# One decoder block on one core: row tile 2's modulation sums move from TensorE to VectorE, and the opening is put in a new order

## The chip, the cores and the metric

The kernel runs on one core of a Trainium2 chip. The metric is the device time of one execution in microseconds (us). Engines are named as the profile names them: PE (TensorE matmuls), PEld (its weight loads), DVE (VectorE), ACT (ScalarE), POOL (GpSimd) and SP (SyncE, which here only issues DMAs, in order).

## The reference, cut to what matters

The block computes six modulation vectors from `c`, normalises and modulates `x`, and multiplies the result by a wide matrix `w_in`; the rest (a state-space branch, attention, a gated merge, an MLP) follows and is not touched by the change.

```python
c_act = jax.nn.silu(c)
mod = c_act @ w_ada[l] + b_ada[l]                     # (1, 6 * 2048)
sh1, sc1, g1, sh2, sc2, g2 = jnp.split(mod, 6)
h = rms_norm(x, norm_mix_g[l]) * (1.0 + sc1) + sh1    # 256 x 2048
proj = h @ w_in[l]                                    # 2048 x (1024 + 3 * 1024 + 2 * 2048)
u, q, k, v, ga, gb = jnp.split(proj, split_at, axis=-1)
```

So no row of `h` exists before its entries of `sc1` and `sh1` do, and each of those entries is a sum over 2048 products of `w_ada` with `silu(c)`. Everything is in float32.

## The kernel before, in words

**Row tiles.** The 2048 model features are cut into 16 row tiles of 128, numbered 0 to 15. Row tile kt of `h` (128 features by 256 tokens, transposed) is made by `make_h1`: ScalarE applies scale `A1[kt]` and shift `B1[kt]` to the normalised `x`, then `split` stores it as a high part (ScalarE's cast, in `ah`) and a low part (VectorE's subtraction, in `al`).

**w_in tiles.** `w_in` is streamed in tiles of 128 x 1024 (512 KB each). A tile is loaded into `wraw` (seven buffers), split into `whi` (ScalarE cast) and `wlo` (VectorE subtraction, four buffers each), and multiplied in three passes: high by high, high by low, low by high. A q, k or u tile is 24 matmuls of 256 columns (`steps_t`, tile name pt, lines 270 to 272); a v or gate tile is 12 of 512 columns (`steps_n`, pn, lines 327 to 331). I count w_in tiles in the order in which the code streams them (`self.tno`): tiles 1 to 4 are q, k, v, u with row tile 0; then `duo` interleaves gate (`gp`) with row tiles 0 to 3 and u with row tiles 1 to 3 (tiles 5 to 11); then v, q with rows 1 to 3, and so on. The last rows, 14 and 15, are first used by tiles 51 and 52.

**Where the sums are made.** For row tiles 0 to 2 the sums run on TensorE: `ada_first` loads two 512 KB pieces of a host-side layout `wan` for the scale and two for the shift, multiplies them in 32-column strips (`adap`, 16 matmuls per vector, each counted twice in the trace since a float32 product runs as two passes), copies the 128 x 128 result to SBUF (`acopy`, ScalarE) and folds it with a ones column (`adac`). For row tile 3 and all later ones they run on VectorE: `ada_wide` loads two 512 KB pieces per row of 128 x 2048 from `wat`, and one instruction multiplies by `cb` (the broadcast `silu(c)`) and accumulates.

**What orders the work.** A planner orders the instructions of each engine by priority and simulated readiness. `high_priority` raises a block (by 300 for the w_in stream, by 3000 for the rows 0 to 3); `after(ins)` puts an instruction behind `ins` on `ins`'s own engine only. `self.gates` holds pairs (VectorE instruction, ScalarE instruction) that the next w_in tiles' splits must follow. `self.last` chains loads on SP. Lanes are lists of jobs, called in `step` after each w_in tile's matmuls: lane "second" (rate 1.0) makes row tiles 1 to 3, lane "ada" (rate 0.75) makes rows 4 to 15, with three empty jobs in front, and `want(kt)` pulls jobs early if row kt has not been written down yet when its first w_in tile is streamed.

In the kernel before, lane "second" fetches row 1 at tiles 3 and 4, sums it on TensorE behind tile 4, makes row 1 and then loads, sums and makes row 2 at tile 5 (sums behind tile 5's last matmul), and sums row 3 on VectorE in the steps after tiles 7 and 8. `ssm_params2` (two sines on ScalarE and some thirty small VectorE instructions) stands at tile 3.

Of the kernel before, what the change touches and what calls it, by code (L numbers as in the profile page):

```python
# [19 lines left out]
P = 128  # L20
# [57 lines left out]
class Kern:  # L78
# [111 lines left out]
    def stream(self, src, kts, c0, homes=()):  # L190
        homes = list(homes)
        kts, nxt = list(kts), None
        for i, kt in enumerate(kts):
            with self.tc.high_priority(offset=OFF):
                w = nxt if nxt is not None else self.load(src, kt, c0)
                nxt = None
                if self.raw:
                    self.raw(w)
                home = homes.pop(0) if homes else None
                if home:  # L200
                    hi, lo = home
                else:
                    hi = self.wp.tile([P, 1024], F32R, name="whi", tag="whi", bufs=4)
                    lo = self.wp.tile([P, 1024], F32R, name="wlo", tag="wlo", bufs=4)
                self.gate, self.hgate = self.gates.pop(0) if self.gates else (None, None)
                self.tno += 1
                if self.pend and self.pend[0][0] <= self.tno - 2:
                    self.gate = self.pend.pop(0)[1]
                self.split(hi, lo, w)
                self.wcast = self.done[-1][1]  # L210
                self.gate = self.hgate = None
                if self.look and i + 1 < len(kts):
                    self.look, nxt = False, self.load(src, kts[i + 1], c0)
# [41 lines left out]
    def steps_t(self, src, kts, c0, xh, xl, koff=0, mid={}, homes=(), seed=None):  # L255
        nc = self.nc
        banks = self.four("pt")
        full = self.seeded(banks, seed)
        n = len(kts)
        for i, (kt, hi, lo) in enumerate(self.flow(src, kts, c0, homes)):  # L260
            kx = kt - koff
            if i in mid:
                mid[i]()
            turn = self.mm if self.strict else None
            for blk in range(8):
                o = banks[blk // 2][:, (blk % 2) * S:(blk % 2 + 1) * S]
                c = slice(blk * P, (blk + 1) * P)
                st, sp = i == 0 and blk % 2 == 0 and not full, i == n - 1
                with self.after(turn):
                    nc.tensor.matmul(o, hi[:, c], xh[:, kx, :], start=st, stop=False, skip_group_check=True)  # L270
                    nc.tensor.matmul(o, hi[:, c], xl[:, kx, :], start=False, stop=False, skip_group_check=True)  # L271
                    self.mm = nc.tensor.matmul(o, lo[:, c], xh[:, kx, :], start=False, stop=sp,  # L272
                                               skip_group_check=True)
                if blk == 3:
                    self.mid = self.mm
            self.whi = hi
            yield banks
# [60 lines left out]
    def ada_first(self, j, kt, done, home=None, gate=None):  # L338
# [14 lines left out]
        def total(i):  # L353
            w = st.pop(i).rearrange("p (k n) -> p k n", k=8)
            if i == 0:
                st["p"] = self.aux("adap")
            p = st["p"][:, 0:P]
            with self.after(self.ss_last if self.early else gate):
                for k in range(8):
                    q = 32 * (k % 4)  # L360
                    m = nc.tensor.matmul(p[q:q + 32, :], self.cz[:, 8 * i + k, :], w[:, k, :], start=i == 0 and k < 4,
                                     stop=i == 1 and k > 3, tile_position=(0, q), skip_group_check=True)
            if i == 1:
                acc = self.s4[:, 512 + P * n:640 + P * n]
                self.acopy = nc.scalar.copy(acc, p)
                st["acc"], st["last"] = acc, m

        def fold(gate=None):
            pc = self.aux("adac")
            with self.after(gate):  # L370
                self.adac = nc.tensor.matmul(pc[:, 0:1], st["acc"], self.ones[:, 0:1], start=True, stop=True)
            done(pc[:, 0:1])
        return ([(lambda i=i: load(i), lambda i=i: total(i)) for i in range(2)], fold, lambda: st["last"])

    def ada_job(self, vec, k0, n, done, ring=None):
# [41 lines left out]
    def ada_wide(self, vec, k0, n, done, ring):  # L417
# [12 lines left out]
        def total(i):  # L430
            w = st.pop(i)
            with self.after(self.lead or self.done[-1][0]), self.after(self.floor):
                sm = v.scalar_tensor_tensor(w, w, 1.0, self.cb, op0=OP.mult, op1=OP.mult, accum_out=pc[:, i:i + 1])
            if k0 >= 8:
                self.pend.append((self.tno, sm))
            if i == n - 1:
                done(pc)
# [183 lines left out]
    def ssm_params(self):  # L621
# [30 lines left out]
        v.scalar_tensor_tensor(em1, ss, -1.0, em1, op0=OP.add, op1=OP.add)  # L652
        self.scan_in = (r, mag, em1, are, aim, tmp)

    def ssm_params2(self):
# [3 lines left out]
        with self.after(self.done[-1][1]):  # L659
            nc.scalar.activation(sh, r, AF.Sin, scale=0.5)  # L660
            nc.scalar.activation(sn, r, AF.Sin)
# [348 lines left out]
    def body(self):  # L1010
# [110 lines left out]
        homes = {1: regs[0:4], 2: regs[4:8]}  # L1121

        sums, h2 = {}, []

# [15 lines left out]
                                tot()  # L1140
            return f

        def third(i):
            def f():
                with self.tc.high_priority(offset=OF1):
                    if i == 0:
                        ring3 = [h.rearrange("p k c -> p (k c)") for h in h4]
                        sums[3] = (self.ada_wide(1, 3, 1, fin_scale(1, A1, lambda: self.gmix, 3, 1), ring3)
                                   + self.ada_wide(0, 3, 1, fin_shift(0, B1, 3, 1), ring3))
                    if i < 2:  # L1150
                        sums[3][i][0]()
                        self.last = self.wide_ld
                    if i:
                        self.lead = h2[0][0] if i == 1 else self.done[-2][0]
                        sums[3][i - 1][1]()
                        self.lead = None
                    if i == 2:
                        self.make_h1(3, A1, B1, 1)
                        self.floor = self.done[-1][0]
                        self.gates = [(self.shifted, None), (self.floor, None)]  # L1160
            return f

        def finish(kt):
            def f():
                with self.tc.high_priority(offset=OF1):
                    for units, fold, last in sums[kt]:
                        fold(sums[kt][1][2]())
                    self.make_h1(kt, A1, B1, 1)
                    self.force = self.adac
                    if kt == 1:  # L1170
                        self.gates += [(self.shifted, self.acopy)]
                    else:
                        h2.append(self.done[-1])
                        self.gates += [(self.shifted, None), h2[0]]
                        self.seedgate = h2[0][1]
            return f

        def params2():
            with self.after(self.done[-1][0]):
                self.ssm_params2()  # L1180

        def both(*fs):
            return lambda: [f() for f in fs]
# [22 lines left out]
        def evac(which, banks, add):  # L1206
# [4 lines left out]
            for b in range(4):  # L1211
# [1 line left out]
                if which == 4 and add:  # L1213
                    d = self.ga[:, b // 2, (b % 2) * 512:(b % 2) * 512 + 512]
                with self.after(self.wcast):
                    nc.scalar.copy(d, view(banks[b]))  # L1216

        g1t = {}

# [51 lines left out]
        self.want = want  # L1271
        nop = lambda: None
        units = []
        wide = [h[:, 2 * i:2 * i + 2, :].rearrange("p k c -> p (k c)") for h in (hv, hq) for i in range(2)]
        ring = wide * 6
        for k0 in range(4, KT, 2):
            units += mod1(k0, 2, ring) + [(None, hjob(k0))]
# [3 lines left out]
        def drain(n):  # L1281
            while len(ready) < n:
                self.lanes["ada"][0].pop(0)()

        self.drain = drain
        self.lane("second", [nop, nop, both(fetch(1, 0), params2), both(fetch(1, 1), follow(1)),
                              both(finish(1), fetch(2, 0), fetch(2, 1), follow(2), finish(2)), third(0), third(1),
                              third(2)], 1.0)
        self.lane("xr", [lambda: self.scale1(1, self.done[-1][0], 3)]
                  + [lambda k0=k0: self.scale1(k0, self.done[-1][0]) for k0 in range(4, KT, 2)], 2.0)  # L1290
        jobs = self.ringed(units, free)
        self.lane("ada", [nop] * 3 + jobs + late, R1)
# [32 lines left out]
        self.cover = True  # L1325
        self.look = True
        qkvu(order[3], order[4])
        duo(order[4], order[5], (0, 0, 0, 1, 1, 0, 1), order[6], lambda: h2[0][1], 4)
        self.cover = False
        qkvu(order[6], order[7])  # L1330
        qkvu(order[7], order[8], True)
# [409 lines left out]
```

## Time and profile before

| | |
|---|---|
| median of 3 runs | 1356.92 us (1356.69 to 1357.32) |
| profiled execution, its own time | 1356.04 us |
| its span, first to last instruction | 1354.3 us |
| PE, DVE, ACT busy | 99%, 77%, 55% of the span |
| mean granted TensorE clock | 0.999 |

The span is what the trace's clock runs over; 1.74 us of the execution's own time lie outside it. Busy time on PE is modelled for pipelined matmuls, so I read PE by the starts of successive matmuls instead: work that issues back to back has equal distances between starts.

### The profile page before, as it was taken

How to read it: one execution, taken by the hardware profiler on the slowest of the kernel's cores; microseconds unless marked ns; L12 is line 12 of the kernel's file. 1: busy time of each engine (PE TensorE's matmuls, PEld its weight loads, DVE VectorE, ACT ScalarE, POOL GpSimd, SP SyncE). 2: the span in 40 equal slices, each digit the busy share in tenths (PEclk: the TensorE clock that was granted, in tenths of full speed). 3: DMA queues.
4: the chain of work that ended last, by engine and by line, in shares of the span. 5: the costliest groups of instructions: out<-in, count | busy, mean ns of one | idle time of the engine just before them, and what ended most of it. 6: DMA issues, size and time to landing. Idle time of an engine off the chain costs nothing.

```text
span 1354.3 us, 21608 instructions
## 1 busy us (share of the span) xinstructions
PE 1342.8 (99%) x8276; PEld 1167.6 (86%) x8276; DVE 1038.2 (77%) x1441; ACT 751.1 (55%) x1045; POOL 49.0 (4%) x105
## 2 busy tenths in 40 slices
PE   9999999999999999999999999999999999999997
PEld 8898899788888988888998888888888888888886
DVE  7888998677987888988888967686765555565687
ACT  7768656766558543455546656353554544535544
POOL 0000004200004000000000000000000000000000
PEclk9999999999999999999999999999999999999999
DMA  9999977975568888997899897888878666566552
GB/s 377 407 408 409 389 252 210 306 241 180 159 215 262 314 283 300 334 337 290 291 342 339 296 235 263 220 281 258 276 243 230 190 187 197 187 188 198 176 196 83
DMA packets 116856, 357.09 MB, mean 264 GB/s; under 512 B 16728, under 2 KB 16864, under 8 KB 116464
## 3 DMA queue, kind: packets, MB, share of 16 engines
q1 hardware_dynamic: 113056, 348.83, 76.5%
q0 software_dynamic: 3120, 5.70, 1.4%
q8 instruction: 65, 1.06, 0.3%
q10 hardware_dynamic: 576, 1.18, 0.3%
q14 instruction: 39, 0.32, 0.1%
HBM read 350.79 MB, written 2.51 MB: 261 GB/s over the span
## 4 chain that ended last, share of the span: by engine, by line
PE 95%; ACT 2%; DMA 2%; DVE 1%; issue 0%; SPq 0%; ACTq 0%; DVEq 0%
PE pn L327 18%; PE pn L329 18%; PE pn L331 18%; PE pd L289 14%; PE pd L293 7%; PE pt L270 6%; PE pt L272 6%; PE pt L271 6%; DMA wraw<-in_w_in_dram 1%; PE ys L992 1%; ACT whi L184 1%; DMA xt<-in_xt_dram 0%; PE trh L834 0%; PE vr L954 0%; PE rk L794 0%
## 5 line engine op out<-in xcount | busy, mean ns | idle before, releaser
L186 DVE TENSOR_TENSOR wlo<-wraw,whi 128x1024 fp32r<-128x1024 f32 x448 | 546.2, 1224 | 254.4 <-ACT whi L184 253.0
L184 ACT CAST whi<-wraw 128x1024 fp32r<-128x1024 f32 (+1 forms) x449 | 467.3, 1051 | 479.6 <-PE pn L329 214.3
L289 PE MATMUL pd<-h2h,whi 128*128 128x512 f32 x800 | 207.3, 393 | 0.2 <-ACT whi L184 0.2
L327 PE MATMUL pn<-whi,ff 128*128 128x512 f32 x496 | 193.3, 390 | 0.0
L329 PE MATMUL pn<-whi,ff 128*128 128x512 f32 x496 | 193.3, 390 | 0.0
L331 PE MATMUL pn<-wlo,ff 128*128 128x512 f32 x496 | 190.9, 390 | 0.0
L289 PEld LDWEIGHTS pd<-h2h,whi 128*128 128x128 f32 x800 | 141.3, 189 | 22.9 <-ACT whi L184 0.4
L391 DVE SCALAR_TENSOR_TENSOR wraw<-wraw,cb 128x1024 f32<-128x1024 f32 x128 | 156.2, 1221 | 0.0
L327 PE MATMUL pn<-whi,ah 128*128 128x512 f32 x320 | 126.7, 400 | 0.8 <-ACT qk L1216 0.4
L329 PE MATMUL pn<-whi,ah 128*128 128x512 f32 x320 | 125.5, 392 | 0.0
L293 PEld LDWEIGHTS pd<-h2h,wlo 128*128 128x128 f32 x800 | 114.8, 190 | 11.5
L293 PE MATMUL pd<-h2h,wlo 128*128 128x256 f32 x800 | 117.9, 282 | 0.0
L331 PE MATMUL pn<-wlo,ah 128*128 128x512 f32 x320 | 115.9, 392 | 0.4 <-DVE wlo L186 0.4
L331 PEld LDWEIGHTS pn<-wlo,ff 128*128 128x128 f32 x496 | 93.1, 188 | 19.5
L329 PEld LDWEIGHTS pn<-whi,ff 128*128 128x128 f32 x496 | 93.2, 188 | 19.0
L327 PEld LDWEIGHTS pn<-whi,ff 128*128 128x128 f32 x496 | 93.1, 188 | 19.1
L270 PE MATMUL pt<-ah,whi 128*128 128x256 f32 x384 | 105.9, 286 | 0.2 <-DVE tz L611 0.2
L271 PE MATMUL pt<-ah,whi 128*128 128x256 f32 x384 | 104.9, 283 | 0.0
L272 PE MATMUL pt<-ah,wlo 128*128 128x256 f32 x384 | 95.9, 284 | 0.8 <-DVE wlo L186 0.7
L270 PEld LDWEIGHTS pt<-ah,whi 128*128 128x128 f32 x384 | 73.4, 192 | 1.8 <-ACT whi L184 0.7
L271 PEld LDWEIGHTS pt<-ah,whi 128*128 128x128 f32 x384 | 73.4, 192 | 0.2
L327 PEld LDWEIGHTS pn<-whi,ah 128*128 128x128 f32 x320 | 59.9, 188 | 15.3 <-ACT whi L184 1.3
(386 smaller groups left out, 2009.3 us busy)
## 6 DMA issues: line engine op xcount, KB each, us to landing
wraw<-in_w_ff_dram SPq DMA_DIRECT2D x256, 512.0 KB, 4.8
wraw<-in_w_in_dram SPq DMA_DIRECT2D x128, 512.0 KB, 6.1
wraw<-in_wat_dram SPq DMA_DIRECT2D x128, 512.0 KB, 5.9
ahm<-in_wat_dram SPq DMA_DIRECT2D x48, 512.0 KB, 10.2
wraw<-in_w_out_dram SPq DMA_DIRECT2D x32, 512.0 KB, 6.5
wraw<-in_w_proj_attn_dram SPq DMA_DIRECT2D x16, 512.0 KB, 5.7
wraw<-in_w_proj_ssm_dram SPq DMA_DIRECT2D x16, 512.0 KB, 6.4
ahm<-in_wan_dram SPq DMA_DIRECT2D x8, 512.0 KB, 10.6
```

The lines of the kernel that those rows point to most:

```text
L184: h = self.nc.scalar.copy(hi[:, c], src[:, c])
L186: s = self.nc.vector.tensor_sub(lo, src, hi.bitcast(F32))
L270: nc.tensor.matmul(o, hi[:, c], xh[:, kx, :], start=st, stop=False, skip_group_check=True)
L271: nc.tensor.matmul(o, hi[:, c], xl[:, kx, :], start=False, stop=False, skip_group_check=True)
L272: self.mm = nc.tensor.matmul(o, lo[:, c], xh[:, kx, :], start=False, stop=sp, skip_group_check=True)
L289: nc.tensor.matmul(banks[blk], hi[:, cut(blk, k)], x2[:, ks[k], :, :], start=i + k == 0, stop=False, skip_group_check=True)
L293: self.mm = nc.tensor.matmul(banks[blk][:, S:2 * S], lo[:, cut(blk, k)], x2[:, ks[k], 0, :], start=False, stop=last and k == 1, skip_group ...
L327: nc.tensor.matmul(o, xh[:, kx, tk], hi[:, c], start=q == 0 and not full, stop=False, skip_group_check=full)
L329: nc.tensor.matmul(o, xl[:, kx, tk], hi[:, c], start=False, stop=False, skip_group_check=full)
L331: self.mm = last = nc.tensor.matmul(o, xh[:, kx, tk], lo[:, c], start=False, stop=q == n - 1, skip_group_check=full)
L391: v.scalar_tensor_tensor(w, w, 1.0, self.cb[:, (i % 2) * 1024:(i % 2 + 1) * 1024], op0=OP.mult, op1=OP.mult, accum_out=pc[:, i:i + 1])
L992: nc.tensor.matmul(p[q, c], self.cc[q, i, j].rearrange("p s c -> p (s c)"), self.sri[q, b % 2, i, c], start=i == 0, stop=False)
```

## The change

- Row tile 2's sums move from `ada_first` (TensorE) to `ada_wide` (VectorE, two instructions over 128 x 2048), with loads from `wat` instead of `wan` (four of 512 KB either way).
- Row 1 is fetched whole at tile 3, and its TensorE sums stand behind tile 3 instead of tile 4. Its copies to SBUF (`bring`) come only at the fold, behind the last evacuation copy (`self.moved`), and its fold stands behind the middle matmul of tile 4 (`self.mid`).
- The VectorE sums of row 2 are put between the splits of tiles 3 and 4 and of tiles 4 and 5; those of row 3 between the splits of tiles 7 and 8, and behind tile 8's. `behind` makes a w_in tile's split wait for the sum in front of it.
- `duo` takes u's row 1 before the gate's row 2. A unit's stored partial results are copied back (`seeded`) after its first w_in tile has been split, not before.
- `ssm_params2`'s sines stay at tile 3; its VectorE part moves to the step in front of tile 10.
- Lane "ada" has six empty jobs in front instead of three.

```diff
@@ stream
-                self.wcast = self.done[-1][1]
+                self.newest, self.wcast = self.done[-1]
@@ steps_t
-        full = self.seeded(banks, seed)
+        full, n = seed is not None, len(kts)
         for i, (kt, hi, lo) in enumerate(self.flow(src, kts, c0, homes)):
+            if i == 0:
+                self.seeded(banks, seed)
@@ ada_first
             if i == 1:
-                acc = self.s4[:, 512 + P * n:640 + P * n]
-                self.acopy = nc.scalar.copy(acc, p)
-                st["acc"], st["last"] = acc, m
+                st["last"] = m
+                if self.early:
+                    bring()
+        def bring(gate=None):
+            acc = st["acc"] = self.s4[:, 512 + P * n:640 + P * n]
+            with self.after(gate):
+                self.acopy = nc.scalar.copy(acc, st["p"][:, 0:P])
-        def fold(gate=None):
+        def fold(gate=None, then=None):
+            if "acc" not in st:
+                bring(self.moved)
...
-            done(pc[:, 0:1])
+            with self.after(then):
+                done(pc[:, 0:1])
@@ ada_wide
+            self.summed = sm
@@ body
+        def bring(kt, j):
+                    if j == 0:
+                        single(kt, wide[2:] if kt == 2 else [h.rearrange("p k c -> p (k c)") for h in h4])
+                    sums[kt][j][0]()
+                    self.last = self.wide_ld
+        def add(kt, j):
+                    self.lead = self.newest
+                    sums[kt][j][1]()
+                    self.lead = None
+        def behind(*gates):
+                self.gates += [g and (self.summed, None) or (None, None) for g in gates]
+        def modulate(kt):
+                    self.make_h1(kt, A1, B1, 1)
+                    h2.append(self.done[-1])
+        def last():
+            modulate(3)()
+            self.floor = self.done[-1][0]
+            self.gates += [(self.floor, None)]
+        def finish():
+                for units, fold, end in sums[1]:
+                    fold(self.mid, self.summed)
+                self.make_h1(1, A1, B1, 1)
+                h2.append(self.done[-1])
+                self.force = self.adac
+                self.seedgate = h2[0][1]
+        def first():
+            self.gates += [h2[0]]
@@ evac
-                    nc.scalar.copy(d, view(banks[b]))
+                    self.moved = nc.scalar.copy(d, view(banks[b]))
@@ lanes
-        self.lane("second", [nop, nop, both(fetch(1, 0), params2), both(fetch(1, 1), follow(1)),
-                              both(finish(1), fetch(2, 0), fetch(2, 1), follow(2), finish(2)), third(0), third(1),
-                              third(2)], 1.0)
+        self.lane("second", [nop, nop, both(fetch(1, 0), fetch(1, 1), follow(1), bring(2, 0), add(2, 0), behind(1),
+                                            angles),
+                             both(bring(2, 1), add(2, 1), behind(1), finish, first), behind(0),
+                             both(bring(3, 0), bring(3, 1), add(3, 0), behind(1), modulate(2)),
+                             both(add(3, 1), behind(0)), both(last, params2)], 1.0)
-        self.lane("ada", [nop] * 3 + jobs + late, R1)
+        self.lane("ada", [nop] * 6 + jobs + late, R1)
-        duo(order[4], order[5], (0, 0, 0, 1, 1, 0, 1), order[6], lambda: h2[0][1], 4)
+        duo(order[4], order[5], (0, 0, 1, 0, 1, 0, 1), order[6], lambda: h2[0][1], 4)
```

More of the change, by code (lines that the diff above doesn't have):

```diff
@@ L257, in steps_t @@
         banks = self.four("pt")
-        full = self.seeded(banks, seed)
-        n = len(kts)
+        full, n = seed is not None, len(kts)
         for i, (kt, hi, lo) in enumerate(self.flow(src, kts, c0, homes)):
             kx = kt - koff
+            if i == 0:
+                self.seeded(banks, seed)
             if i in mid:
@@ L653, in ssm_params, with ssm_angles @@
         self.scan_in = (r, mag, em1, are, aim, tmp)
+    def ssm_angles(self):
+        r, tmp = self.scan_in[0], self.scan_in[-1]
+        with self.after(self.wcast):
+            self.nc.scalar.activation(tmp(10), r, AF.Sin, scale=0.5)
+            self.nc.scalar.activation(tmp(11), r, AF.Sin)
     def ssm_params2(self):
@@ L658, in ssm_params2 @@
         sh, sn = tmp(10), tmp(11)
-        with self.after(self.done[-1][1]):
-            nc.scalar.activation(sh, r, AF.Sin, scale=0.5)
-            nc.scalar.activation(sn, r, AF.Sin)
         v.tensor_mul(sh, sh, sh)
@@ L1120, in body @@
         regs = [h[:, i, :] for h in (hv, hq) for i in range(4)]
-        homes = {1: regs[0:4], 2: regs[4:8]}
+        homes = {1: regs[0:4]}
+        wide = [h[:, 2 * i:2 * i + 2, :].rearrange("p k c -> p (k c)") for h in (hv, hq) for i in range(2)]
         sums, h2 = {}, []
@@ L1141, in follow, with single @@
             return f
-        def third(i):
+        def single(kt, ring):
+            sums[kt] = (self.ada_wide(1, kt, 1, fin_scale(1, A1, lambda: self.gmix, kt, 1), ring)
+                        + self.ada_wide(0, kt, 1, fin_shift(0, B1, kt, 1), ring))
+        def bring(kt, j):
             def f():
                 with self.tc.high_priority(offset=OF1):
[L1146 to L1160, printed above, removed]
@@ L1161, in third @@
+                    if j == 0:
+                        single(kt, wide[2:] if kt == 2 else [h.rearrange("p k c -> p (k c)") for h in h4])
+                    sums[kt][j][0]()
+                    self.last = self.wide_ld
             return f
-        def finish(kt):
+        def add(kt, j):
             def f():
                 with self.tc.high_priority(offset=OF1):
-                    for units, fold, last in sums[kt]:
-                        fold(sums[kt][1][2]())
-                    self.make_h1(kt, A1, B1, 1)
[L1169 to L1175, printed above, removed]
-            return f
+                    self.lead = self.newest
+                    sums[kt][j][1]()
+                    self.lead = None
+            return f
@@ new lines, in behind, with f @@
+        def behind(*gates):
+            def f():
+                self.gates += [g and (self.summed, None) or (None, None) for g in gates]
+            return f
+        def modulate(kt):
+            def f():
+                with self.tc.high_priority(offset=OF1):
+                    self.make_h1(kt, A1, B1, 1)
+                    h2.append(self.done[-1])
+            return f
+        def last():
+            modulate(3)()
+            self.floor = self.done[-1][0]
+            self.gates += [(self.floor, None)]
@@ L1178, in params2 @@
+        def finish():
+            with self.tc.high_priority(offset=OF1):
+                for units, fold, end in sums[1]:
[6 more added lines that the diff above has]
+            self.gates += [h2[0]]
         def params2():
-            with self.after(self.done[-1][0]):
+            with self.after(self.newest):
@@ L1180, in params2, with angles @@
                 self.ssm_params2()
+        def angles():
+            with self.after(self.newest):
+                self.ssm_angles()
         def both(*fs):
@@ L1273, in body @@
         units = []
-        wide = [h[:, 2 * i:2 * i + 2, :].rearrange("p k c -> p (k c)") for h in (hv, hq) for i in range(2)]
         ring = wide * 6
```

## The prediction

> **What bounds the kernel now.** I read the page first, then the busy times of a few stretches, then the order of PE's matmuls and of SP's loads in the opening. The page's first line and its chain of work:
>
> ```profile
> span 1354.3 us, 21608 instructions
> ```
>
> ```profile
> PE 95%; ACT 2%; DMA 2%; DVE 1%; issue 0%; SPq 0%; ACTq 0%; DVEq 0%
> ```
>
> The chain that ends last is matmuls, so an edit pays if it takes work or waits out of PE's queue, and only as long as PE doesn't then wait for something else. What that could be shows in the stretches (each engine's busy us, then PE clock, DMA share, GB/s):
>
> ```profile
> 27.60:57.40 29.80, 29.40 (x285) 25.48 (x284) 22.95 (x47) 21.44 (x39) 0.52 (x1) 1.00 1.03 406
> ...
> 66.00:165.00 99.00, 98.96 (x684) 92.01 (x683) 89.81 (x98) 67.44 (x102) 1.04 (x2) 1.00 1.03 408
> 165.00:1354.30 1189.30, 1180.53 (x7072) 1020.71 (x7070) 895.10 (x1197) 634.20 (x863) 45.32 (x89) 1.00 0.75 245
> ```
>
> The reader is to see three things. All that is edited runs between 27.6 and 57.4, where VectorE is idle for 29.80 - 22.95 = 6.85 us. To 165 us the DMA moves 406 to 408 GB/s without a pause, and from 66 to 165 VectorE has only 9 us in 99 to spare. Behind 165 the DMA falls to 245 GB/s and PE alone sets the time, so a lead that PE still has at 165 lasts to the end. The granted clock is 1.00 throughout.
>
> **PE's part.** The groups of PE's instructions from 27.6 to 57.4 that aren't products with w_in (count, busy us, mean ns), and its instructions in order of time:
>
> ```profile
> L361 PE MATMUL adap<-ahm,tz 128*32 128x128 f32 x128 | 3.9, 274 | 0.0
> L371 PE MATMUL adac<-s 128*128 128x1 f32 x8 | 1.1, 208 | 0.0
> L115 PE MATMUL pt<-ah 128*128 128x512 f32 x3 | 1.1, 419 | 0.0
> ```
>
> ```profile
> 27.59 0.28 PE L270 MATMUL pt<-ah,whi 128*128 128x256 f32 x1
> ...
> 36.09 1.95 PE L361 MATMUL adap<-ahm,tz 128*32 128x128 f32 x64
> 37.97 0.96 PE L327 MATMUL pn<-whi,ah 128*128 128x512 f32 x3
> 38.77 0.28 PE L371 MATMUL adac<-s 128*128 128x1 f32 x2
> 38.91 0.48 PE L329 MATMUL pn<-whi,ah 128*128 128x512 f32 x1
> ...
> 49.76 0.39 PE L272 MATMUL pt<-ah,wlo 128*128 128x256 f32 x1 [0.29 <-DVE wlo L186]
> ...
> 51.77 1.09 PE L327 MATMUL pn<-whi,ah 128*128 128x512 f32 x4
> ...
> 54.52 0.28 PE L270 MATMUL pt<-ah,whi 128*128 128x256 f32 x1
> ...
> 57.39 0.40 PE L327 MATMUL pn<-whi,ah 128*128 128x512 f32 x1
> ```
>
> The 128 adap passes are rows 1 and 2; row 2's 64 hold PE from 36.09 to 37.97, 1.88 us. Its two folds cost 38.91 - 38.77 = 0.14 each, 0.28. Each of these three breaks also restarts the full-width matmuls; the first after such a break takes about 0.1 us more than its neighbours by the spacing of starts, which I put at 0.3 together. **Removed from PE: 1.9 + 0.3 + 0.3 = about 2.4 us.** Row 1's 64 passes only move from behind u's tile 4 to behind v's tile 3.
>
> From the same rows, a v or gate tile takes 54.52 - 51.77 = 2.75 us and a q, k or u tile 57.39 - 54.52 = 2.87 us.
>
> **SP's part.** The moved loads decide when tiles 4 and 5 land. SP's loads in order (start, time of the issues, name, count), and the time from issue to landing of row 3's loads, with the sum on VectorE that reads them:
>
> ```profile
> 8.99 1.61 SPq L349 DMA_DIRECT2D ahm<-in_wan_dram  x2
> 13.22 0.33 SPq L176 DMA_DIRECT2D wraw<-in_w_in_dram  x1
> 13.60 0.91 SPq L349 DMA_DIRECT2D ahm<-in_wan_dram  x2
> 15.44 3.31 SPq L176 DMA_DIRECT2D wraw<-in_w_in_dram  x2
> 19.55 4.11 SPq L349 DMA_DIRECT2D ahm<-in_wan_dram  x4
> ...
> 32.33 2.89 SPq L176 DMA_DIRECT2D wraw<-in_w_in_dram  x3
> 36.17 0.33 SPq L427 DMA_DIRECT2D ahm<-in_wat_dram  x1
> ```
>
> ```profile
> L433 DVE SCALAR_TENSOR_TENSOR ahs<-ahs,cb x2: 2285/2286/2286, 42.4 to 46.2; 128x2048 f32<-128x2048 f32 x2
> ...
> DMA to landing us min/median/max: 10.2/10.2/10.2
> ```
>
> Four issues take 4.11 us, the last 0.33 of it by itself: one 512 KB load each 1.26 us, the pace of the full DMA. Counted from 8.99, before has row 1 twice, tile 4, row 1 twice, tiles 5 and 6, and row 2 as loads 8 to 11 from 19.55. After, the fetch of row 1 and row 2's scale stand at priority 3000 in one step ahead of tile 4: row 1 as 1 to 4, row 2's scale as 5 and 6, tile 4 as 7, row 2's shift as 8 and 9, tiles 5, 6, 7 as 10 to 12, then row 3. With load 8 at 19.55, 10.2 to land and 1.26 between loads, row 2's scale is there at 27.2, tile 4 at 28.5, row 2's shift at 31.0, tile 5 at 32.3, tile 6 at 33.5. The bytes are the same, so the DMA gains or loses nothing; tile 4 is five microseconds later than before.
>
> ```profile
> 25.00 1.05 ACT L184 CAST whi<-wraw 128x1024 fp32r<-128x1024 f32 x1
> ```
>
> That is tile 4's cast now; 1.05 us is its price. After, tile 4 is cast by 29.55 and tile 5 by 33.35.
>
> **VectorE's part.** It gains two sums of 2.29 us, 4.6 us, in a stretch with 6.85 us idle. Both have landed when their place comes: row 2's scale is summed from 27.2 to 29.5, tile 4's split follows to 30.7; the shift is summed from 31.0 to 33.3, row 1's few scalars and tile 5's split follow to about 35. `ssm_params2`'s small operations move from the front of this stretch to its end, cost nothing while the idle time lasts, and would delay tile 10's split if it didn't. ScalarE loses two copies and has 29.80 - 21.44 = 8.4 us idle; the later `seeded` copies find their split done. POOL's bias load waits for a buffer that `ssm_params2` now holds longer, and nobody needs it in the opening.
>
> **The sum.** PE ends tile 3 at 27.59 as before; row 1's sums (landed long before) take it to 29.6, just when tile 4 has been cast; tile 4 to 32.4. Then it waits for tile 5's cast until 33.4, about 0.95 us: the one new wait. From there four gate tiles and three u tiles, 4 x 2.75 + 3 x 2.87 = 19.6, and the three L115 matmuls, about 0.8, without a wait: 53.8, with row 1's folds 53.9. Before that point stood at 57.39, so 3.5 us are gained: 2.4 of work, and the waits like that at 49.76, which vanish because their sums come earlier, less the new one. I take 0.3 off for first low-part matmuls that catch their split too soon: **3.2 us**.
>
> The new waits have no row of their own, so I bound them. If PE runs each tile's blocks strictly high, high, low, tile 4's first low matmul stands at 29.9 and waits to 30.7, and tile 5's stands at 33.9 and waits to 35.1: 2.0 us more, a gain of 1.2. If tile 5 has no wait at all (SP puts it ahead of row 2's shift), 4.4. I take the value near the upper end, since the row at 51.77 shows four high matmuls ahead of the first low one: PE's order already puts high parts first where a split is late.
>
> **Does the lead last to 165?** The tightest places of the DMA and of the last rows, in ScalarE's, VectorE's and PE's order:
>
> ```profile
> 160.30 1.05 ACT L184 CAST whi<-wraw 128x1024 fp32r<-128x1024 f32 x1 [2.79 <-DMA wraw<-in_w_in_dram]
> ```
>
> ```profile
> 165.04 0.69 DVE L186 TENSOR_TENSOR ah<-htmp,ah 128x512 fp32r<-128x512 f32 x1
> ```
>
> ```profile
> 166.12 0.39 PE L327 MATMUL pn<-whi,ah 128*128 128x512 f32 x1
> ...
> 171.56 0.39 PE L327 MATMUL pn<-whi,ah 128*128 128x512 f32 x1
> ```
>
> Tile 49's cast waits for its DMA, ends at 161.35 and is used at 166.12: a margin of 4.8 us. Rows 14 and 15 are done at 165.73 and used at 171.56 (tile 51): 5.8 us. A lead of 3.2 fits into both. The three extra empty jobs cost nothing at the front: row 4's first load stands at 36.17, directly behind tiles 9 to 11 (32.33, three loads), where the new place puts it too. At the back the list is pulled by `want`; writing both lists out, the last sum comes one tile later (behind tile 49's split instead of 48's) and rows 14 and 15 two, of which two times 2.8 less the lead still fits.
>
> In the profiled execution: span 1354.3 - 3.2 = 1351.1, its own time 1356.04 - 3.2 = 1352.8. The median of the runs lies 0.9 above that execution, so 1356.92 - 3.2 = **1353.7 us**. A change of 0.2%, 2.7 us, is about what a measurement of this kernel tells from none.
>
> **The rivals.** *Waits take the place (within 0.2%).* Tiles 4 and 5 wait for forced sums as in the lower bound: 1.2 us gained, 1355.7. For it speaks the wait at 49.76, where a split behind a sum did hold PE; against it, that PE had its high parts in front there and lost 0.29 only. The Trainium skill ("TensorE: Matmul & The Clock Gate", section "Architectural detail: the array is 16× 32×32, not 1× 128×128") says that VectorE's queue is strictly first in, first out; by that rule everything queued behind a sum whose row is late waits too, and no row here shows a sum that waited for its row.
>
> *The DMA is the bound (no change).* It is full to 165 us, so PE's lead is given back as w_in tiles stop landing in time: 1356.9. For it: 406 to 408 GB/s throughout and the 2.79 us wait of tile 49's cast. Against it: that cast is still 4.8 us ahead of PE, and the loads in front of it are the same. The Trainium skill ("Perfetto Trace Analysis", section "Identifying the Most-Contended Engine") has the engine with the highest occupancy, for DMA its share of the bandwidth, set the time; with the 435 GB/s that "DMA: Bandwidth & Descriptors", section "Where 436 GB/s comes from", gives as the ceiling, 408 is 94%, and the sum by that rule would be zero. I weigh it below the 4.8 us that the rows show in hand.
>
> *The later rows come too late (slower).* If the three empty jobs really shift every later sum by four tiles (three at 0.75 a tile), 4 x 2.87 = 11.5 us, rows 14 and 15 are ready at 165.73 + 11.5 = 177.2 against 171.56, and PE stands 5.7 us at tile 51: 1362.6. It decides from 5.8 us of delay on; half of the shift is a draw. For it: VectorE's 9 us spare in 99, and sums bound to the newest split. Against it: `want` and the one-tile count above.
>
> **How the numbers follow.** The forecast (2.2 to 4.4 gained, 1352.5 to 1354.7) has 0.62, of which 0.50 lies beyond 2.7 us; waits 0.13; DMA 0.12; late rows 0.13. So faster 0.50, within 0.2% 0.12 + 0.13 + 0.12 = 0.37, slower 0.13. The range: at the low end tile 49's whole margin is used, 1356.9 - 4.8 - 0.3 (the spread of the runs) = 1351.8; at the high end rows come 7.3 us late, 1.5 beyond the draw, 1358.4.
>
> **What would show it.** Right: row 2's adap and adac gone from PE, its two sums on VectorE before 34; tile 4's cast near 28.5; PE 3 us or more ahead at tile 12 (57.39 before) and still at tile 51 (171.56). Wrong: waits of PE over 0.5 us on `wlo` at tiles 4 to 8; a lead that shrinks between 66 and 165 with casts released by DMA; PE waiting for `ah` at tile 25 or 51.

## The result: slower by 0.6%, and the profile after

| | before | after |
|---|---|---|
| time, median of the runs (us) | 1357.06 (1355.58 to 1357.51) | 1365.27 (1364.35 to 1366.52) |
| span of the profiled execution (us) | 1354.3 | 1363.8 |

The ratio is 1.0062, with a 95% interval of 1.0049 to 1.0075: 8.2 us slower in the runs, 9.5 in the two profiled spans. Forecast were 3.2 us faster.

The opening itself went as forecast. The end of tile 11 and the next two tiles, in PE's order of time after the change:

```profile
54.03 0.28 PE L273 MATMUL pt<-ah,wlo 128*128 128x256 f32 x1
55.15 0.50 PE L328 MATMUL pn<-whi,ah 128*128 128x512 f32 x1 [0.84 <-ACT pn L237]
...
59.63 0.50 PE L328 MATMUL pn<-whi,ah 128*128 128x512 f32 x1 [1.40 <-ACT whi L184]
```

Tile 11's last matmul starts at 54.03, where 53.9 was forecast for the end of the tile. Its matmuls start 0.12 us apart, so tile 12 could start at 54.15; before, it started at 57.39. PE has a lead of about 3.2 us (0.35 of it already stood at tile 3, at 22.45 against 22.80). The bracket of the next line is the first bad sign: PE waits where it did not wait before. All waits of PE from 27 to 110 us (total, number, longest):

```profile
PE pt L272 <- DVE ah L186: 3.4, 1, 3.4
PE pt L271 <- ACT ah L184: 2.7, 1, 2.7
PE pn L328 <- ACT whi L184: 1.7, 2, 1.4
PE pn L328 <- ACT pn L237: 0.8, 1, 0.8
```

One `whi` wait, 0.3 us, is at tile 6 (36.81). The rest is in two places, read by the spacing of the matmuls: 2.6 us at tiles 12 and 13, and 6.3 us (2.8 and 3.5) for `ah` at tile 21, the first tile that needs rows 4 and 5.

**The first place.** SP's loads behind tile 11's, before and after the change (start, time of the issues, count), then ScalarE after it:

```profile
36.17 0.33 SPq L427 DMA_DIRECT2D ahm<-in_wat_dram  x1
37.44 0.33 SPq L176 DMA_DIRECT2D wraw<-in_w_in_dram  x1
38.73 5.59 SPq L427 DMA_DIRECT2D ahm<-in_wat_dram  x5
```

```profile
30.16 4.59 SPq L176 DMA_DIRECT2D wraw<-in_w_in_dram  x4
35.71 6.68 SPq L436 DMA_DIRECT2D ahm<-in_wat_dram  x6
43.39 0.33 SPq L176 DMA_DIRECT2D wraw<-in_w_in_dram  x1
```

```profile
53.56 1.05 ACT L184 CAST whi<-wraw 128x1024 fp32r<-128x1024 f32 x1 [0.71 <-DMA wraw<-in_w_in_dram]
54.52 2.14 ACT L237 COPY pn<-v 128x512 f32<-128x512 f32 x4
56.60 2.03 ACT L1249 COPY uT<-pt 128x512 f32<-128x512 f32 x4
58.51 2.02 ACT L184 CAST whi<-wraw 128x1024 fp32r<-128x1024 f32 x2
```

Tile 12's load stood at 37.44, behind one load of row 4 and ahead of five more; now it stands at 43.39, behind all six, and its cast waits for it until 53.56. PE's wait at 55.15 is for the first of the copies `pn<-v` (L237) behind that cast: these are the stored partial results, which the change copies back only after the unit's first split. Tile 13's cast stands behind tile 12's and eight copies, at 58.51.

**The second place.** VectorE, before and after: the sums (L433, L442) of rows 4 and 5, and the last subtraction for `ah` that these rows need.

```profile
53.56 2.29 DVE L433 SCALAR_TENSOR_TENSOR ahm<-ahm,cb 128x2048 f32<-128x2048 f32 x1
...
62.74 2.28 DVE L433 SCALAR_TENSOR_TENSOR ahm<-ahm,cb 128x2048 f32<-128x2048 f32 x1
...
76.68 0.69 DVE L186 TENSOR_TENSOR ah<-htmp,ah 128x512 fp32r<-128x512 f32 x1
```

```profile
54.64 1.23 DVE L186 TENSOR_TENSOR wlo<-wraw,whi 128x1024 fp32r<-128x1024 f32 x1 [2.04 <-ACT whi L184]
59.61 2.36 DVE L186 TENSOR_TENSOR wlo<-wraw,whi 128x1024 fp32r<-128x1024 f32 x2 [3.74 <-ACT whi L184]
61.89 2.28 DVE L442 SCALAR_TENSOR_TENSOR ahm<-ahm,cb 128x2048 f32<-128x2048 f32 x1
...
73.14 2.28 DVE L442 SCALAR_TENSOR_TENSOR ahm<-ahm,cb 128x2048 f32<-128x2048 f32 x1
...
88.94 0.68 DVE L186 TENSOR_TENSOR ah<-htmp,ah 128x512 fp32r<-128x512 f32 x1
```

No load makes these sums late: the six stand at 35.71 to 42.4, about where they stood, and a load lands some 10.2 us after its issue. But the first sum runs at 61.89 in place of 53.56, and VectorE is idle for 2.04 and 3.74 us ahead of it. Six empty jobs put the first sum behind the step of tile 14, and `done[-1]` then binds it to tile 14's split. The last subtraction moves from 76.68 to 88.94, 12.3 us. PE's second wait there is for it: ScalarE has cast its operand by 85.50, but in VectorE's order a split (85.59) and a sum (86.73) stand ahead of it. PE and its clock there (each engine's busy us, then PE clock, DMA share, GB/s):

```profile
85.56 0.74 PE L271 MATMUL pt<-ah,whi 128*128 128x256 f32 x4 [2.68 <-ACT ah L184]
89.68 0.58 PE L272 MATMUL pt<-ah,whi 128*128 128x256 f32 x1 [3.38 <-DVE ah L186]
```

```profile
82.60:85.50 2.90, 0.28 (x3) 0.08 (x1) 2.90 (x2) 2.90 (x5) 0.00 (x0) 1.00 1.02 401
85.50:89.70 4.20, 0.76 (x5) 0.56 (x5) 4.19 (x7) 0.00 (x1) 0.00 (x0) 0.61 1.04 415
89.70:93.40 3.70, 3.70 (x17) 3.70 (x18) 0.16 (x1) 0.00 (x0) 0.00 (x0) 0.52 1.02 407
93.40:97.00 3.60, 3.60 (x33) 3.60 (x32) 2.08 (x2) 1.34 (x2) 0.00 (x0) 1.00 1.02 406
```

A further cost comes with the gap: the granted clock is 0.52 from 89.7 to 93.4. There 17 matmuls fit where 33 fit in the next 3.6 us: one starts every 0.21 us, not every 0.12, and 17 x 0.09 is about 1.5 us more.

The same as a ledger. The ends of four units (the end of ScalarE's copies of them, us; other columns: difference to before) show where each kernel stands:

| unit's end, before | after | 3 jobs | before, 6 jobs | sums early | both repairs | less PE work |
|---|---|---|---|---|---|---|
| 56.45 | -3.6 | +5.2 | -0.6 | -3.7 | -3.6 | -1.8 |
| 59.43 | -0.8 | +6.6 | -0.6 | -0.5 | -1.7 | -1.8 |
| 75.93 | -0.1 | +4.9 | +0.2 | -0.5 | -0.7 | -1.3 |
| 101.37 | +9.1 | +4.2 | +5.9 | +4.6 | -0.9 | -1.4 |
| span, 1354.3 | +9.5 | +4.5 | +4.9 | +3.6 | +2.4 | -1.0 |

The last unit's end overstates the loss after the change: ScalarE makes that unit's four copies in pieces there, the last at 109.86, where before all four stand together at 99.31; PE's next change from `pt` to `pn` matmuls is 7.6 us late (113.91 against 106.31). PE's own starts are the safer measure:

| start on PE, before | after | 3 jobs | before, 6 jobs | sums early | both repairs | less PE work |
|---|---|---|---|---|---|---|
| tile 3, 22.80 | -0.4 | -0.6 | -0.6 | -0.6 | -0.6 | -0.2 |
| tile 49, 163.38 | +7.2 | +5.3 | +4.0 | +2.9 | +0.5 | -1.4 |
| first `pn` matmul behind 235, 238.81 | +6.8 | +5.4 | +4.0 | +2.5 | +0.8 | -1.4 |

The first row shows how far single executions differ: the opening of the kernel before, unedited in the columns *before, 6 jobs* and *less PE work*, is 0.6 and 0.2 us earlier there. After the change the lead is nearly gone by tile 21, some 8 us are lost there, and 6.8 stand at 239. **A third place** comes behind that, 2.7 of the 9.5 us of span:

```profile
268.00 0.49 PE L873 MATMUL sco<-qk 128*128 128x128 f32 x2 [2.51 <-ACT bp L777]
```

```profile
265.37 1.04 ACT L184 CAST whi<-wraw 128x1024 fp32r<-128x1024 f32 x1 [3.05 <-DMA wraw<-in_w_in_dram]
```

PE waits for four small copies (`bp`) that ScalarE makes at 266.44, behind a cast that waited for its load; before the change ScalarE makes them at 259.35 and PE does not wait. The size of this wait is not fixed by the order of the work: run 4 below, which differs only by matmuls at tile 21, has 0.2 us there. So a difference of two spans can hold some 2 us of this place, beside what tile 21 costs. The other columns are the runs that follow.

### The profile page after: what moved, and what is told of

Its sections match the earlier page's. It is cut to its first block, busy times and chain, and to the rows that moved or that the text cites. A ratio compares the mean times of both kernels' runs of the same rounds, so it can differ in the third digit from the quotient of the medians.

```text
span 1363.8 us, 21476 instructions
## 1 busy us (share of the span) xinstructions
PE 1341.7 (98%) x8208; PEld 1165.5 (85%) x8208; DVE 1041.5 (76%) x1445; ACT 751.7 (55%) x1043; POOL 49.0 (4%) x105
## 4 chain that ended last, share of the span: by engine, by line
PE 91%; DMA 6%; ACT 1%; DVE 1%; issue 0%; SPq 0%; ACTq 0%; DVEq 0%
PE pn L328 17%; PE pn L330 17%; PE pn L332 17%; PE pd L290 13%; PE pd L294 7%; PE pt L272 5%; PE pt L273 5%; PE pt L271 5%; DMA wraw<-in_w_in_dram 3%; DMA ahm<-in_wan_dram 1%; DMA rt<-cmp 1%; DMA wraw<-in_wat_dram 1%; PE ys L1005 1%; DMA wraw<-in_wan_dram 1%; ACT whi L184 1%
## 5 line engine op out<-in xcount | busy, mean ns | idle before, releaser
L273 PE MATMUL pt<-ah,wlo 128*128 128x256 f32 x384 | 100.3, 287 | 0.5 <-DVE wlo L186 0.4
```

## The experiments

Time in each is given as the ratio to the kernel before on the same chip, with its 95% interval.

**1 and 2. Three or four empty jobs in place of six, in the changed kernel.**

```
-        self.lane("ada", [nop] * 6 + jobs + late, R1)
+        self.lane("ada", [nop] * 3 + jobs + late, R1)      (2: [nop] * 4)
```

> The changed kernel with three empty jobs at the head of the list of row sums, as before the change, in place of six; nothing else is undone. Theory (the late sums): the sums of rows 4 and 5 come four tiles later than before because each is bound behind the newest split, so PE stands 2.8 + 3.5 us at tile 21 for `ah`, and its clock falls behind that gap. Then this kernel has no wait over 1 us on `ah` at tile 21, a granted clock of 1.00 from 66 to 165, and takes 8 to 11 us less than the changed kernel: 1354 to 1357; the waits of about 1 and 1.6 us at tiles 12 and 13 may stay. Rival (the front: row 2's sums on VectorE, the forced places or the order of the loads are to blame): the wait at tile 21 stays or moves to another tile, and the time is 1363 or more.

> The changed kernel with four empty jobs at the head of the list of row sums, one more than before the change. Theory (the late sums): each empty job shifts the sums of rows 4 and 5 by one tile or a little more, about 2.9 us, against a margin of about 5.9 us that these rows had before the change (tile 21 starts at about 83.3, the rows are done at 77.4). One job more uses half of it: no wait over 0.5 us on `ah` at tile 21, the same time as with three jobs within 1 us, 1354 to 1358. Rival (the front is to blame): 1363 or more, as with six jobs. A third reading (the number of jobs only moves the loads, and the loads are what is late): a time halfway, about 1360, with casts released by DMA at tiles 11 to 14.

Measured: 1.0050 (1.0031 to 1.0069) and 1.0046 (1.0031 to 1.0061), 1362.3 and 1362.9 us; spans 1358.8 and 1360.0. The wait at tile 21 is gone in both, as the theory said, but most of the time is not back. SP, ScalarE and PE with three jobs:

```profile
34.33 6.68 SPq L436 DMA_DIRECT2D ahm<-in_wat_dram  x6
42.01 0.33 SPq L176 DMA_DIRECT2D wraw<-in_w_in_dram  x1
```

```profile
52.29 1.99 ACT L184 CAST whi<-wraw 128x1024 fp32r<-128x1024 f32 x2 [4.31 <-DMA wraw<-in_w_in_dram]
```

```profile
53.38 0.79 PE L328 MATMUL pn<-whi,ah 128*128 128x512 f32 x1 [4.79 <-ACT whi L184]
```

The six row loads now stand ahead of tile 10's load, which PE needs at 48.4, and PE waits 4.8 us there. So the theory was half right: sums that are early enough need loads that are early, and in the new opening, with PE about 3 us ahead, those loads push a tile out. My expectation of 1354 to 1357 had not looked at SP's order. The rival (the wait moves to another tile, 1363 or more) and the third reading of run 2 (casts released by DMA) came nearer.

**3. Six empty jobs in the kernel before, its opening untouched** (the same edit the other way round, 3 to 6).

> The kernel before the change with six empty jobs at the head of the list of row sums in place of three; its opening is untouched. Theory (the late sums): the same shift of the sums of rows 4 and 5 by about four tiles, 4 x 2.87 = 11.5 us at most, against a margin of 5.9: PE waits at tile 21 for `ah`, some 3 to 5 us, and the clock may fall behind it; 1360 to 1364. Rival (the list has slack and only the new opening uses it up): no wait at tile 21, 1357 as before. By the text on record (the extra empty jobs cost nothing) it is 1357 too.

Measured: 1.0041 (1.0028 to 1.0054), span 1359.2. PE's waits from 30 to 110, and VectorE ahead of the first sum:

```profile
PE pt L271 <- DVE ah L186: 2.6, 1, 2.6
PE pt L272 <- DVE wlo L186: 0.3, 1, 0.3
```

```profile
59.81 2.36 DVE L186 TENSOR_TENSOR wlo<-wraw,whi 128x1024 fp32r<-128x1024 f32 x2 [6.76 <-ACT whi L184]
62.09 2.29 DVE L433 SCALAR_TENSOR_TENSOR ahm<-ahm,cb 128x2048 f32<-128x2048 f32 x1
```

SP's loads of rows 4 and 5 stand in the order of the kernel before, so this run shows the sums alone. The one constant costs 4.9 us of span by itself, 4.0 of it by tile 49: the first sum at 62.09 in place of 53.56, VectorE idle for 6.76 us ahead of it, PE 2.6 us at tile 21 and a low clock behind. The prediction's sentence that the extra empty jobs cost nothing is refuted.

**4. Matmuls in the gap at tile 21.** 28 matmuls of 512 columns whose result nobody reads, ahead of tile 21.

```
+            if kt == 4 and c0 == 1024 and self.warm:
+                for _ in range(self.warm): ...matmul(o, self.ah[:, 0, 0:P], self.a2[:, 0]...)
```

> The changed kernel with 28 additional matmuls of 512 columns, whose result nobody reads, in front of the first tile that needs row 4 (tile 21). They cost about 28 x 0.24 = 6.7 us of PE at a place where PE stands 6.3 us idle. Theory (the gap itself costs about 6.3 us, and the granted clock of 0.5 to 0.6 in the 8 us behind it costs another 1.4 to 1.8 us): the clock stays at 1.00 from 82 to 100, and the time falls by 1 to 1.8 us, to about 1363.5 to 1364.3. Rival (the clock shown behind the gap costs nothing, PE is waiting there anyway): 1365 to 1366.

Measured: 1.0057 (1.0036 to 1.0078), span 1361.0 against 1363.8. The changed kernel from 82 to 100, then this run:

```profile
82.00:100.00 18.00, 11.94 (x85) 11.54 (x84) 12.63 (x15) 6.92 (x11) 0.00 (x0) 0.81 1.03 409
82.00:100.00 18.00, 18.00 (x126) 16.73 (x125) 12.58 (x15) 7.67 (x12) 0.00 (x0) 1.00 1.03 409
```

The clock stays at 1.00 where it was 0.81 over the same stretch, and the unit that ended 9.1 us late ends 7.9 us late. PE starts tile 49 at 169.41, not 170.60, also 1.2 us less: about so much the low clock is worth in the traces. The rest of the shorter span goes with the smaller wait at the third place (0.2 for 2.5). The runs' interval is too wide to tell any of it.

**5. Only the sums of rows 4 and 5 earlier**, loads and six jobs as changed.

```
-            with self.after(self.lead or self.done[-1][0]), self.after(self.floor):
+            with self.after(self.lead or self.done[-4 if k0 == 4 else -1][0]), self.after(self.floor):
```

> The changed kernel, in which only the four sums of rows 4 and 5 are bound to a split three tiles older than the newest; the six empty jobs and the first loads of these rows stay. VectorE's order then has these rows' last subtraction behind tile 19's split, as before the change, and no longer behind tile 24's. Theory (two separate losses: 2.6 us at tiles 12 and 13, whose loads stand behind six row loads, and 6.3 us plus a low clock at tile 21, whose rows are summed late): the waits at 54 and 58 stay, the one at tile 21 and the low clock go; span 1363.8 - 6.3 - 1.5 = about 1356, time about 1357 to 1358. Rival (the lead that PE lost at tiles 12 and 13 isn't what counts; VectorE has no room for the sums in front of tile 21): PE waits for `wlo` at tiles 12 to 20 instead, and the time stays over 1361.

Measured: 1.0022 (1.0013 to 1.0032), span 1357.9. The only edit is where four sums stand on VectorE, and by tile 49 it brings back 4.3 of the 7.2 us (of the span 5.9 of 9.5, 1.5 of it at the third place; by the runs, 0.62% of slowdown falls to 0.22%). PE's waits from 30 to 110:

```profile
PE pt L271 <- ACT ah L184: 1.7, 1, 1.7
PE pn L328 <- ACT whi L184: 1.4, 1, 1.4
PE pn L328 <- ACT pn L237: 1.2, 1, 1.2
```

The waits at 54 and 58 stay, the one at tile 21 is gone, and a new one of 1.7 us comes at 94.2: the next pair, rows 6 and 7, whose sums are still late. I had not expected it; the span is 1.9 us longer than I expected.

**6. Only the loads spread**: SP's order becomes four row loads, tile 12, two row loads, tiles 13 and 14.

```
-        free = {None: ((0, 1), (2,), (3,))}
+        free = {None: ((0,), (1,), (2,), (3,))}
```

> The changed kernel, in which only the first four loads of rows 4 and 5 come in four jobs of one in place of two, one, one: SP's order is then tile 11, four row loads, tile 12, two row loads, tiles 13 and 14, two row loads, in place of tile 11, six row loads, tile 12, two, tile 13. All sums come one tile later. Theory: tile 12 lands by about 51 in place of 53.6, the waits at 54 and 58 go (2.6 us), and PE then waits so much longer at tile 21 (2.6 for the lead, 2.8 for the sum that is a tile later): about 10 to 12 us there, and 1364 to 1368 in all; nothing gained at the front survives. Rival (the front wait is what costs): 1362 to 1363.

Measured: 1.0093 (1.0078 to 1.0108), span 1365.1, with these waits from 30 to 110:

```profile
PE pt L271 <- ACT ah L184: 5.5, 2, 2.8
PE pt L272 <- DVE ah L186: 3.3, 1, 3.3
PE pn L328 <- ACT whi L184: 1.4, 1, 1.4
```

Tile 12's wait is gone, tile 13's stays, and nothing of it survives: PE waits at tile 21 again, and 2.8 us more at 101.8 for the next pair of rows. I had put all of the delay at tile 21, 10 to 12 us; it is 6 there. The median, 1368.8, is a little above the 1364 to 1368 that I expected.

**7 and 8. Both repairs.** Loads as in 6 with the sums of rows 4 and 5 bound four splits further back and those of rows 6 and 7 three (`done[-5]`, `done[-4]`); in 8 an empty job between the first two loads, and sums one split further back again, those of rows 8 and 9 now among them.

> The loads of the run before (four jobs of one) with the sums of rows 4 and 5 bound to a split four tiles older than the newest and those of rows 6 and 7 three tiles older. VectorE's order has rows 4 and 5 behind tile 19's split, rows 6 and 7 behind tile 25's (before the change 19 and 24). Theory: neither the waits at tiles 12 and 13 nor the one at tile 21; PE keeps 2 to 3.4 us of its lead to 95, and perhaps 2 to 165, where the full DMA takes the rest: 0 to 2 us faster than before the change, about 1354 to 1356. Rival (the DMA is the bound to 165 and gives back every lead): the same as before the change, with waits for `whi` or `ah` spread from 60 to 165.

> As the run before, with one empty job between the first and the second load (SP's order: tile 11, two row loads, tile 12, two, tiles 13 and 14, two, tile 15, two) and the sums bound one tile older still. VectorE's order has rows 4 and 5 behind tile 18's split, rows 6 and 7 behind tile 25's, rows 8 and 9 behind tile 31's (32 before the change). Theory: the same as the run before within 1 us, since neither the tiles' loads nor the rows are late in either; if PE waited for `whi` at tiles 13 to 15 in the run before, that wait is gone here. Rival (sums forced so early hold up VectorE's queue, because their rows have not landed): waits for `wlo` at tiles 12 to 16, slower by 1 us or more.

Measured: 1.0017 (1.0008 to 1.0027) and 1.0021 (1.0012 to 1.0031), spans 1356.7 and 1356.4. In 7, from 30 to 110, only this is left of the waits:

```profile
PE pn L328 <- ACT whi L184: 1.4, 1, 1.4
```

So two orders, six loads ahead of a tile and sums behind the newest split, explain 6.7 of the 7.2 us by which PE was late at tile 49; of the span 7.1 of 9.5 are back. In 8 that wait is 0.8, and waits of 1.2 and 0.4 us on `wlo` end at 65.8 and 69.3, behind sums that stand further forward: the rival of 8 in small. The theory of both had 0 to 2 us faster than before the change; neither is.

**9 and 10. What is a lead worth?** In the kernel before, the product with the inputs' low part is left out (9) or made twice (10) in the first four gate tiles; all loads and sums keep their places.

```
+                            for _ in range(0 if c0 == 4096 and kt < 4 else 1):      (10: 2)
                                 nc.tensor.matmul(o, xl[:, kx, tk], hi[:, c], start=False, stop=False, ...)
```

> The kernel before the change without the product of the inputs' low part with w_in's high part in the first four gate tiles (between 38 and 55 us): 16 matmuls of 512 columns, 16 x 0.23 = 3.7 us of PE left out, so the gate is a little less exact. The orders of SP and VectorE from tile 8 on stay as before. This gives PE about the lead of the changed kernel at tile 12 (3.5) with nothing else moved. Text on record (the lead lasts to 165 and then to the end): 3 to 3.7 us faster, about 1352.5. Theory now (loads and row sums stay where they are, and the margins read with the right tile numbers are 2.0 at tile 49 and 3.1 at tile 51): at most 2 us stay, 1354 to 1355. Rival (DMA and VectorE to 165 take the whole lead back): within 0.7 us of before.

> The kernel before the change, in which the same product is made twice in the first four gate tiles: 16 matmuls of 512 columns or 3.7 us of PE more at the same place, orders as before. Theory now (PE is busy without a pause from 66 to 165 before the change, so what it loses at 55 it can't catch up): the whole 3.7 us, about 1359.5, more if PE's lateness pushes later casts together. Rival (the DMA sets the time to 165, and PE has slack against it): less than 1.5 us slower.

Measured: 9: 0.9990 (0.9981 to 0.9999), span 1353.3; 10: 1.0021 (1.0012 to 1.0030), span 1358.4. In 9 PE's waits from 30 to 110 were 0.3 us before and are now:

```profile
PE pn L332 <- DVE wlo L186: 1.7, 1, 1.7
PE pn L327 <- ACT whi L184: 1.1, 1, 1.1
```

Of 3.7 us taken from PE, 1.6 are left at 56.45 (measured against the 0.2 by which the two profiles already differ at 24 to 32 us), since PE now waits at tile 7; 1.1 stand to 240, and the span is 1.0 shorter. A small lead does last, then, as the theory had it (at most 2), and the 3 to 3.7 by the prediction's reasoning is refuted: a lead of 3 is not to be had at this place with the tiles' loads where they are. In 10 the 3.7 us more cost 1.9 by the same reckoning until 210, not the whole that I expected: the kernel before had time to spare in the opening. Its tiles 8 and 9, with the wait at 49.76, take 6.7 us there (45.08 to 51.77) and 5.8 in 10. The span is 4.1 longer; 1.2 of that is a wait at 214.6 that the profile puts down to nothing but PE's own issue, and its cause stays open.

**11 and 12. A last try.** Both repairs, and one job (12: 0.9) per tile in place of 0.75, with nine (12: eight) empty jobs and the sums bound anew, so that rows 8 to 15 stand about where they stood before the change.

> The changed kernel with both repairs and a faster list: four single loads at the head as in the runs above, nine empty jobs in place of six, one job per tile in place of three per four tiles up to rows 8 and 9, the sums of rows 4 and 5 bound to a split three tiles older and all others two tiles older than the newest. SP's order is tile 11, four row loads, tile 12, two, tile 13, two, tile 14; the last subtractions of the rows stand behind tiles 19, 23, 31, 38, 44, 50 (before the change 19, 24, 32, 37, 44, 50; with both repairs above 19, 25, 33, 39, 45, 51). Theory: the run with both repairs lost its lead between 107 and 175 because rows 8 to 15 stood a tile later there than before the change. With them in the old place PE keeps about 1.5 to 2 us: span 1352.5 to 1354, 0.5 to 2 us faster than before. Rival (the full DMA and VectorE, 92 to 94% busy from 110 to 165, take every lead): 0 to 2 us slower than before.

> As the run before, with eight empty jobs, 0.9 jobs per tile, the sums of rows 4 and 5 bound five splits back and those of rows 6 and 7 four. SP's order is tile 11, two row loads, tile 12, two, tile 13, two, tile 14, two, tile 15; the rows' last subtractions stand behind tiles 18, 25, 31, 38, 44, 50. Theory: within 1 us of the run before; a difference would come from rows 6 and 7 (two tiles later here): PE waits for `ah` at tile 25, up to 1 us. Rival as for the run before: 0 to 2 us slower than before the change.

Measured: 1.0014 (1.0005 to 1.0022) and 1.0019 (1.0010 to 1.0028), spans 1354.5 and 1356.8; the runs of 11 lie between 1355.75 and 1359.91, its profiled one near the lower end. From 30 to 110 PE still waits there 1.4 us for `whi` (58.66) and 1.2 for `wlo` (66.62).

The rival held for 11 (0.14%, 1.9 us slower); 12, with 2.6, lies a little beyond it. By the unit's end at 101.37, 0.2 and 0.7 us of the lead are left, and none at the `v` unit near 120. No version with the new opening is faster than the kernel before.

## Why the prediction was wrong, point by point

- **PE's part, SP's order in the opening, VectorE's part:** right. Row 2's products and folds are gone, its sums run at 26.35 and 30.19, tile 4 is cast at 27.57 (28.5 forecast), tile 11's last matmul starts at 54.03 (53.9 for its end). The sum for the opening, 3.2 to 3.5 us, was sized right, to some 0.3 us, though one term was not: the wait of 0.95 us for tile 5's cast did not come. Its terms for PE add to 2.5, not 2.4.
- **"The three extra empty jobs cost nothing at the front":** the step that failed. I looked at the place of row 4's first load, which indeed does not move, and not at the sums, which are bound behind the newest split, nor at the five loads behind that first one, which now stand ahead of tile 12's. Run 3 prices the sums at 4.9 us of span with the old opening (4.0 at tile 49); run 5 gives 5.9 us (4.3) back in the new one.
- **"A lead of 3.2 fits into both" margins:** failed twice. First, I looked at the last rows and tiles, 14 and 15 at tile 51, and not at the first rows that the edit delays, 4 and 5 at tile 21, where 12.3 us of delay met some 6 us of margin (76.68 + 0.7 against about 83.3). Second, the margins were read one tile late. Up to 163.4 us PE's trace before the change holds 672 matmuls of 256 columns in q, k and u tiles, 24 for each of 28, and 240 of 512 in v and gate tiles, 12 for each of 20: just 48 tiles. PE starts tile 49 at 163.38, not 166.12, and tile 51 at about 168.8, not 171.56; the margins are 2.0 and 3.1 us, not 4.8 and 5.8. By these the forecast's own rule would have left 2 us at most; run 9 left about 1.
- **Nothing was said of tiles 12 and 13.** The walk of PE ended at tile 11 and took the lead to 165 as given. The first tiles behind it lost 2.8 us of it: tile 12's load had moved behind five row loads, 5.95 us later, and its cast waited for it. With row loads early a tile is late (runs 1, 2), with the sums late the rows are (3, 6), and with both put right PE still waits for ScalarE and VectorE, 1.4 us at tile 13 first (7, 11). That these waits are all that takes the rest of the lead was not tested by a run.
- **The rivals.** *The later rows come too late* was the mechanism, given 0.13 and 1362.6 us; its place was wrong (tile 51) and so were its price and the point from which it decides. Its 11.5 us of delay is what the first rows met (12.3). The stated range left it out: its upper end stood for 7.3 us of delay. *The DMA is the bound* may fit what is left when that is mended, but it is not shown: PE's waits in runs 7 and 11 are for ScalarE's casts and VectorE's splits. *Waits take the place* at tiles 4 and 5 did not come about. The Trainium skill's rule quoted there ("TensorE: Matmul & The Clock Gate", section "Architectural detail: the array is 16× 32×32, not 1× 128×128"), that VectorE's queue is strictly first in, first out, agrees with this trace: the subtraction at 88.94, whose operand was cast by 85.50, ran behind the split and the sum ahead of it in the order. A sum that waits for its row did come, 0.76 us at 26.35, and cost next to nothing: the cast for the split behind it ended at 28.62, and the split began at 28.76.
- **"What would show it":** waits on `ah` were named, at tiles 25 and 51; they came at tile 21.
- **"PE alone sets the time" behind 165:** not quite. PE waits 2.5 us there in the changed kernel, at 268.

What stays open: why PE waits for the `bp` copies ahead of `sco` at about 260 to 268, from 0.2 to 2.5 us, in the changed kernel and in runs 2 to 8 and 12, and not in the kernel before or in runs 1, 9, 10 and 11; and whether tile 13's cast can be put ahead of the copies on ScalarE was not tried.

## What to carry to other kernels

When a list of background jobs is moved, follow each job, and every load of it, to the first consumer, not the last: the first load may not move at all while the loads behind it pass a tile and the sums move by the whole shift, and an engine's idle time right ahead of a late job (here 6.76 us on VectorE) is a sign that a binding and not a resource holds it. A lead is worth only what the next loads and casts can feed; take a little work out of the busy engine at that place first, as run 9 did, and see what reaches the end. Check a count of tiles against a second engine, such as the splits on VectorE: one tile of error was 2.7 us of margin here. And follow PE by its own starts; the end of another engine's copies can lie 1.5 us off.

## What the hardware showed that was not expected

PE's granted clock fell behind gaps much shorter than the 6.3 us at tile 21. In run 5 PE stood idle for 1.9 us at 94.2 (by the spacing of the matmuls):

```profile
94.20:96.10 1.90, 0.25 (x3) 0.04 (x1) 0.00 (x0) 1.90 (x3) 0.00 (x0) 1.00 1.03 412
96.10:99.50 3.40, 3.33 (x16) 3.14 (x17) 3.35 (x4) 0.02 (x1) 0.00 (x0) 0.59 1.02 407
99.50:103.00 3.50, 3.50 (x29) 3.50 (x29) 3.50 (x4) 2.10 (x4) 0.00 (x0) 0.91 1.03 405
```

The next 3.4 us ran at 0.59: 16 matmuls where full speed fits about 29, so a wait of 1.9 us cost some 1.5 more. In run 6 a gap of 2.8 us did not lower it:

```profile
101.80:104.70 2.90, 0.27 (x3) 0.07 (x1) 0.00 (x0) 2.65 (x4) 0.00 (x0) 1.00 0.93 283
104.70:108.00 3.30, 3.27 (x25) 3.08 (x26) 3.29 (x4) 0.00 (x0) 0.00 (x0) 1.00 0.81 318
```

The Trainium skill ("TensorE: Matmul & The Clock Gate", section "HAM oscillation — how this bites in real kernels") gives the rule that PE must not idle for more than about 3.4 us. Run 6's 2.8 us without a drop agree with it, and run 5 differs: 1.9 us were enough there. So in these traces the length of a gap alone does not tell whether the clock falls.
